# Block products with seven multiplications for three of five down-projection steps of the last layer's second token group

## The chip, the cores and the metric

The kernel runs on one core of one Trainium2 chip. The metric is the device time of one execution in microseconds (us): the median of several runs of the whole program, which is one launch.

## What is computed

The reference is one inference step of a two-layer decoder, D_MODEL = 1024, for a prompt of 1024 tokens and 8 sample tokens that share all weights. Layer 0 mixes by a gated linear recurrence and by attention to 256 memory tokens; layer 1 by stick-breaking attention over one shared K/V and by memory attention. After each mixer comes a SwiGLU feed-forward network with D_FF = 2816. All of it is float32.

```
h = h + rmsnorm(mix, g[1])
h = h + rmsnorm(swiglu(rmsnorm(h, g[2]), w_gu[l], w_down[l]), g[3])
```

Here `swiglu(x, w_gu, w_down)` is `(silu(x @ gate) * (x @ up)) @ w_down`. The change concerns the product with `w_down`, (2816, 1024), in layer 1.

## The kernel before

Tokens run in two groups along the free axis: group 0 has 512 prompt tokens, group 1 has the other 512 and the 8 sample tokens, 520 columns. Activations are held transposed, 128 features by tokens. A float32 product is made of three matmuls: each operand is split into a high part, rounded by a copy on ACT, and the rest, subtracted on DVE, and high x high, high x low and low x high are added in PSUM (`split_w` L256 for weights, `split_to` L286 for activations). So each weight block costs one load on SP's queue (256 KB for four blocks of 128x128), one cast on ACT, one subtraction on DVE, and its matmuls.

The order of the work is written by hand as generators: `weave` (L234) takes steps of several streams in the ratio of their weights, `drain` runs one after another. A planner then walks the program in that priority and places each instruction on its engine's queue when it judges it ready and a buffer of its pool free; queues run in order on the chip. Buffers rotate within a tag: `wraw` and `wspl` 5 each for loaded and split weights, tag "t" 3, tag "n" 2, tag "b" 7, "m" 5, the small tag "rr" 3, and from L1627 on four PSUM tags q0 to q3 with 2 banks each.

The feed-forward network works through the 22 blocks of D_FF in five parts of 5, 5, 4, 4 and 4 (`PARTS`, L642): the gate/up products of a part, then its share of the down projection, added into R.

The **last part** of the program is `ffn_w` (L644) for layer 1, group 1, started at L1628 and drained at L1629 and L1630. It splits the 520 columns into halves of 260. Four blocks are done plainly (`gate_up_q`, L528); the other 18 by `gate_up_w` (L553), which takes the gate and up weights as a 2 x 2 block matrix against the two column halves and needs seven block products in place of eight (the Winograd form of Strassen's scheme). Four of the seven use sums of weight blocks. These are made in DRAM ahead of time by `weight_sums` (L617): 8 steps for each part, each a small ACT copy of a value that the running work produces (a token), a POOL copy of the token, and a POOL-issued DMA from DRAM to DRAM that copies or accumulates. Steps are woven at L1606 and L1607 beside layer 1's first group. The sums of the activations are made by `sums_w` (L355). The sum of one product is carried to the next in PSUM by a negating ACT copy (L588, L591), and DVE combines (L599, L601).

The down projection of a part (L689 to L705) goes over the 8 output blocks: `split_w` for the 4 or 5 weight blocks, then for each block three matmuls on each half (L696), then two additions into R from PSUM on DVE (L705), or two copies in part 0 (L703). That is 192 or 240 matmuls of 260 columns a part.

The **recurrence** that the change touches is `a1.core()` (L1355, `hgrn_prompt` L1213), layer 0 group 1, woven at L1589 with part 0 of layer 0's network for group 0. `ffn` (L717) keeps its latest result as `self.now` for tokens.

At the start of the program the masks are built through buffers of tag "t" (L167), and the page table is loaded into a buffer of its own (L210, L211); it is used for indirect loads (L1018) in layer 1.

Of the kernel before, what the change touches and what calls it, by code (L numbers as in the profile page):

```python
# [9 lines left out]
F32 = mybir.dt.float32  # L10
# [8 lines left out]
P = 128  # L19
# [5 lines left out]
def tile_decoder(  # L25
# [50 lines left out]
    def T(dt=F32):  # L76
        return tpool.tile([P, WID], dt, tag="t", name=nm("t"))
# [20 lines left out]
    def M(dt=F32):  # L98
        return mpool.tile([P, 2, WID], dt, tag="m", name=nm("m"))
# [21 lines left out]
    def small(shape, dt=F32, tag="sm", bufs=None):  # L121
        return spool.tile(shape, dt, tag=tag, name=nm(tag), bufs=bufs)
# [86 lines left out]

    ptb = const.tile([P, NB * NP], I32, name="ptb")  # L210
    nc.sync.dma_start(ptb, page_table.rearrange("b j -> (b j)").partition_broadcast(P))  # L211
# [13 lines left out]
    def drain(*gens):  # L225
        for g_ in gens:
            for _ in g_:
                pass
# [5 lines left out]
    def weave(*streams):  # L234
        drain(mixed(*streams))
# [50 lines left out]
    def split_to(dst, src):  # L286
        nc.scalar.copy(dst[0], src)  # L287
        nc.vector.tensor_sub(dst[1], src, dst[0].bitcast(F32))  # L288
# [263 lines left out]

    def gate_up_w(l, f, ops, spl, raws):  # L553

# [37 lines left out]
        product(pa, 3)  # L592
        sg = T()
        nc.scalar.activation(sg[:, :h], pa[:, :h], AF.Silu)
# [10 lines left out]
        nc.vector.tensor_mul(sg[:, h:n], sg[:, h:n], gt[:, h:n])  # L605
        mt = M(F32R)
        split_to((mt[:, 0, :n], mt[:, 1, :n]), sg[:, :n])
        return mt

# [6 lines left out]

    def weight_sums(l, parts, after):  # L617

        for i in parts:
            f0, nf = PARTS[i]  # L620
            w = nf * P
            s1, s2, s3, s4 = (tc.dram_tile([512, w], F32, name=nm("wsum")) for _ in range(4))
            sums.setdefault(l, {})[i] = (s1, s2, s3, s4)
            a11, a12 = (w_gu[l][r : r + 512, f0 * P : f0 * P + w] for r in (0, 512))
            a21, a22 = (w_gu[l][r : r + 512, DFF + f0 * P : DFF + f0 * P + w] for r in (0, 512))
            for d, a, add in (
                (s3, a11, False), (s1, a21, False), (s3, a21, True), (s1, a22, True),
                (s2, s3, False), (s2, a22, True), (s4, s2, False), (s4, a12, True),
            ):
                tok = small([P, 1], tag="rr")  # L630
                nc.scalar.copy(tok, after())
                mark = nc.gpsimd.tensor_copy(small([P, 1], tag="mk", bufs=1), tok)
                with tc.issue_after(mark.ins):
                    if add:
                        nc.gpsimd.dma_start(d, a, accum_op=ALU.add)
                    else:
                        nc.gpsimd.dma_start(d, a, max_dma_last_dim=4 * w)
                yield

    htok = []  # L640

    PARTS = [(0, 5), (5, 5), (10, 4), (14, 4), (18, 4)]  # L642

    class ffn_w:  # L644


        def __init__(self, l, x, plain):
            self.g, self.l, self.x, self.ops, self.plain, self.n, self.r, self.pi = 1, l, x, [], plain, 0, 0, 0
            self.R = self.acc = None
            self.half = []  # L650
            self.sums = sums_w(x, self.ops)
# [15 lines left out]

        def part(self, pi):
            l, n, h = self.l, NG[1], PW[1]
            f0, nf = PARTS[pi]  # L670
            last = pi == len(PARTS) - 1
            mids = []
            for j in range(nf):
                self.pi = pi
                if f0 + j < self.plain:
                    mt, ins = gate_up_q(l, f0 + j, self.x)
                    mids.append(mt)
                    with tc.issue_after(ins.ins):
                        for _ in range((1, 2, 1, 0)[j]):
                            next(self.sums, None)  # L680
                else:
                    mids.append(gate_up_w(l, f0 + j, self.ops, self.spl, self.raws))
                yield
            if pi == 0:
                self.R = R_one()
            if last:
                self.acc = small([P, WID], tag="st", bufs=3)
                nc.scalar.preload_act_table_set("natural_log_exp_and_others")
            for m in range(ND):  # L689
                w = split_w(w_down[l], f0, nf, m * P)  # L690
# [897 lines left out]
    f0 = ffn(0, 0, o0.x)  # L1588
    weave((a1.core(), 22), (f0.part(0), 9))  # L1589
    a1.open()  # L1590
# [72 lines left out]
```

## Time and profile before

| | us |
|---|---|
| median of 3 runs | 2450.96 |
| lowest, highest run | 2450.86, 2453.5 |
| profiled execution | 2454.44 |
| its span in the trace | 2452.7 |

The profile is of one execution; its span is what the instructions cover, and 1.74 us of its time lie around it. Engines are PE (matmul), PEld (weight load, beside PE), DVE, ACT, POOL and SP, which issues loads. A busy PE may wait in its pipeline, so the pace of its matmuls is read beside its share. In the last part `q<-x,ws` and `q<-y,ws` at L581 are gate/up products and `q<-m,ws` at L696 is the down projection; L571/L572 and L266/L267 are cast and subtraction of the weight split.

### The profile page before, as it was taken

The numbers are of one execution on the slowest core, as the hardware profiler recorded it, in microseconds if no ns is written. First come the engines' busy times: TensorE is split into PE (matmuls) and PEld (weight loads), VectorE is DVE, ScalarE is ACT, GpSimd is POOL, SyncE is SP. The second block draws the span as 40 slices with busy tenths as digits, with TensorE's granted clock in tenths as the row PEclk, the third lists the DMA queues.
The fourth block names the chain that finished last, engine by engine and source line by source line (L and its number), as shares of the span: only waits on it lengthen the run. The fifth ranks groups of instructions, "written<-read, shape, count | busy, mean of one in ns | idle before, by whom it ended". The sixth has DMA issues, their size and how long they took to land.

```text
span 2452.7 us, 40619 instructions
## 1 busy us (share of the span) xinstructions
PE 2413.9 (98%) x15473; PEld 2141.9 (87%) x15473; DVE 1563.8 (64%) x2697; ACT 1204.3 (49%) x2354; POOL 102.6 (4%) x153
## 2 busy tenths in 40 slices
PE   7999999999999999999999999999999999999998
PEld 5888988888877887999999989877787898999997
DVE  5777556765775676555544585677677558655665
ACT  4547544444444454555433454555454445564444
POOL 2000000000000000011111100022000000000000
PEclk9999999999999999999999999999999999999998
DMA  5353252263543446686688866453453244375541
GB/s 177 106 157 104 74 159 84 65 178 118 179 136 95 138 146 210 171 221 150 181 201 220 237 187 189 153 163 118 140 154 117 82 126 125 117 200 148 151 134 66
DMA packets 496726, 360.33 MB, mean 147 GB/s; under 512 B 19181, under 2 KB 443738, under 8 KB 496530
## 3 DMA queue, kind: packets, MB, share of 16 engines
q1 hardware_dynamic: 477970, 303.19, 41.2%
q0 software_dynamic: 18560, 54.53, 9.1%
q8 instruction: 122, 2.00, 0.3%
q14 instruction: 74, 0.61, 0.1%
HBM read 327.83 MB, written 75.96 MB: 165 GB/s over the span
## 4 chain that ended last, share of the span: by engine, by line
PE 90%; DVE 4%; DMA 2%; ACT 2%; issue 1%; SPq 0%; POOL 0%; DVEq 0%; ACTq 0%; POOLq 0%
PE mm L280 62%; PE q L581 7%; PE q L696 5%; PE q L539 2%; PE mm L1082 2%; PE s L932 1%; PE s L891 1%; PE s L1265 1%; PE mm L868 1%; PE s L1440 1%; PE mm L841 1%; DMA b<-qd 1%; PE s L1479 1%; PE s L918 1%; DVE ws L267 1%
## 5 line engine op out<-in xcount | busy, mean ns | idle before, releaser
L280 PE MATMUL mm<-x,ws 128*128 128x260 f32 (+1 forms) x7776 | 1330.4, 330 | 0.0
L280 PEld LDWEIGHTS mm<-x,ws 128*128 128x128 f32 x7776 | 1149.2, 188 | 142.9 <-issue 8.2
L266 ACT CAST ws<-w 128x512 fp32r<-128x512 f32 x712 | 420.1, 591 | 685.7 <-PE mm L280 563.6
L267 DVE TENSOR_TENSOR ws<-w,ws 128x512 fp32r<-128x512 f32 x712 | 462.1, 652 | 263.3 <-ACT ws L266 255.7
L280 PE MATMUL mm<-m,ws 128*128 128x512 f32 (+1 forms) x2112 | 393.1, 343 | 0.4 <-DVE r L476 0.4
L280 PEld LDWEIGHTS mm<-m,ws 128*128 128x128 f32 x2112 | 324.3, 189 | 47.3 <-issue 3.4
L696 PE MATMUL q<-m,ws 128*128 128x260 f32 x1056 | 128.8, 283 | 0.0
L696 PEld LDWEIGHTS q<-m,ws 128*128 128x128 f32 x1056 | 127.2, 188 | 0.4 <-ACT hT L514 0.2
L572 DVE TENSOR_TENSOR ws<-w,ws 128x512 fp32r<-128x512 f32 x126 | 86.5, 691 | 59.7 <-ACT ws L571 57.0
L581 PE MATMUL q<-y,ws 128*128 128x260 f32 x864 | 112.9, 283 | 0.0
L571 ACT CAST ws<-w 128x512 fp32r<-128x512 f32 x126 | 78.0, 621 | 67.9 <-PE q L696 27.4
L581 PEld LDWEIGHTS q<-y,ws 128*128 128x128 f32 x864 | 107.6, 188 | 0.0
L476 DVE TENSOR_TENSOR r<-r,mm 128x512 f32<-128x512 f32 (+1 forms) x96 | 66.0, 687 | 59.9 <-PE mm L280 58.8
L320 DVE TENSOR_SCALAR t<-mm 128x512 f32<-128x512 f32 (+1 forms) x74 | 51.2, 692 | 64.3 <-PE mm L280 64.3
L732 DVE TENSOR_TENSOR t<-t,mm 128x512 f32<-128x512 f32 (+1 forms) x66 | 45.5, 689 | 67.9 <-PE mm L280 67.4
L324 DVE TENSOR_TENSOR t<-t,t 128x512 f32<-128x512 f32 (+1 forms) x66 | 45.8, 694 | 65.7 <-ACT t L323 65.7
L581 PE MATMUL q<-x,ws 128*128 128x260 f32 x648 | 86.3, 282 | 0.0
L581 PEld LDWEIGHTS q<-x,ws 128*128 128x128 f32 x648 | 81.3, 188 | 0.0
L343 DVE TENSOR_TENSOR st<-st,n 128x512 f32<-128x512 f32 (+1 forms) x98 | 67.1, 691 | 6.5 <-ACT n L342 5.0
L287 ACT CAST m<-t 128x512 fp32r<-128x512 f32 (+1 forms) x88 | 54.9, 624 | 25.3 <-DVE t L732 16.5
L1018 POOL DMA_INDIRECT c<-in_cache_sb_k,pidx x16 | 16.4, 1026 | 1128.7 <-issue 919.7
L288 DVE TENSOR_TENSOR m<-t,m 128x512 fp32r<-128x512 f32 (+1 forms) x88 | 60.9, 692 | 2.6 <-ACT m L287 1.4
(356 smaller groups left out, 2513.0 us busy)
## 6 DMA issues: line engine op xcount, KB each, us to landing
w<-in_w_gu SPq DMA_DIRECT2D x334, 256.0 KB, 3.1
w<-in_w_down SPq DMA_DIRECT2D x160, 256.0 KB, 2.7
w<-in_w_in_a SPq DMA_DIRECT2D x80, 256.0 KB, 2.9
wsum<-in_w_gu POOLq DMA_DIRECT2D x18, 1024.0 KB, 8.9
w<-wsum SPq DMA_DIRECT2D x72, 256.0 KB, 3.5
w<-in_w_o SPq DMA_DIRECT2D x64, 256.0 KB, 2.7
wsum<-in_w_gu POOLq DMA_DIRECT2D x12, 1280.0 KB, 10.5
w<-in_w_mem_kv SPq DMA_DIRECT2D x32, 256.0 KB, 3.2
```

Of the source, the lines that this page charges most:

```text
L266: nc.scalar.copy(ws[:, 0, :n, :], raw[:, :n, :])
L267: nc.vector.tensor_sub(ws[:, 1, :n, :], raw[:, :n, :], ws[:, 0, :n, :].bitcast(F32))
L280: nc.tensor.matmul(ps[:, a, : PW[g]], wt, xt[k][:, xi, o : o + PW[g]], start=(k == 0 and wi == 0), stop=(k == nk - 1 and wi == 2),)
L287: nc.scalar.copy(dst[0], src)
L288: nc.vector.tensor_sub(dst[1], src, dst[0].bitcast(F32))
L320: nc.vector.tensor_scalar(sv(x, g), pv(ps, g), -44.0, None, op0=ALU.max)
L343: nc.vector.tensor_add(acc[:, :n], acc[:, :n], t[:, :n])
L476: nc.vector.tensor_add(dst, dst, pv(ps, g))
L571: nc.scalar.copy(w[:, 0, :], src)
L572: nc.vector.tensor_sub(w[:, 1, :], src, w[:, 0, :].bitcast(F32))
L581: nc.tensor.matmul(ps[:, :h], w[:, wj, k * P : (k + 1) * P], x[:, xi, :], start=(first and k == 0 and wi == 0), stop=(k == 3 and wi == 2), ...
L696: nc.tensor.matmul(pp[a][:, :h], wt, mids[k][:, xi, a * h : (a + 1) * h], start=(k == 0 and wi == 0), stop=(k == nf - 1 and wi == 2),)
```

## The change

For parts 1, 2 and 3 the down projection also takes seven block products. The four weight blocks of a part form a 2 x 2 block matrix: rows by the parity of the block (blocks 0 and 2, blocks 1 and 3), columns by the halves of the 1024 outputs; the activations form one by parity and by column halves. `down_w` does this in two groups of two output blocks for each half of the outputs, holding all eight PSUM banks; a product is 12 matmuls, fed by one 256 KB load and one split. The fifth block of part 1 is added plainly (`slice_of`). Results go into R by DVE additions, 12 in a group and 14 with the fifth block, and two negating ACT copies of two banks each join the products.

The sums of down weights are made in DRAM by `down_sums`, 24 token steps of 512 KB, woven beside the recurrence at L1589. The sums of activations are made by `gate_up_w` for pairs of blocks: the first of a pair splits half 0 and the difference of the halves, the second splits itself and three more sums (`put_sum`: a subtraction, an ACT cast, a subtraction, 260 columns each). One of part 3's gate/up steps now comes ahead of part 2's down projection, and one of part 4's ahead of part 3's. The gate/up sums of the four plain blocks of part 0 are left out. The page table and its index go through buffers of tag "t".

```diff
-    ptb = const.tile([P, NB * NP], I32, name="ptb")
+    ptb = tpool.tile([P, NB * NP], I32, tag="t", name="ptb")
...
-    iot = const.tile([P, NB * NP], I32, name="iot")
+    iot = tpool.tile([P, NB * NP], I32, tag="t", name="iot")
...
-    def gate_up_w(l, f, ops, spl, raws):
+    def gate_up_w(l, f, ops, spl, raws, pair=None):
...
-        sg = T()
+        sg = T() if pair is None else N()
...
         mt = M(F32R)
+
+        def put_sum(dst, d, a, b):
+            nc.vector.tensor_sub(d, a, b)
+            split_to((dst[:, 0], dst[:, 1]), d)
+
+        if not pair:
+            w = n if pair is None else h
+            split_to((mt[:, 0, :w], mt[:, 1, :w]), sg[:, :w])
+            if pair is not None:
+                put_sum(mt[:, :, h:n], sg[:, :h], sg[:, h:n], sg[:, :h])
+                pair.append((mt, sg))
+            return mt
+        m0, s0 = pair.pop()
         split_to((mt[:, 0, :n], mt[:, 1, :n]), sg[:, :n])
+        y = [bpool.tile([P, 2, h], F32R, tag="b", name=nm("ys")) for _ in range(3)]
+        put_sum(y[2], s0[:, h:n], s0[:, h:n], sg[:, h:n])
+        put_sum(y[1], sg[:, h:n], sg[:, h:n], s0[:, :h])
+        put_sum(y[0], sg[:, :h], sg[:, :h], sg[:, h:n])
+        pair.extend((m0[:, :, :h], mt[:, :, :h], mt[:, :, h:n], y[0], m0[:, :, h:n], y[1], y[2]))
         return mt
...
-    def weight_sums(l, parts, after):
+    def weight_sums(l, parts, after, plain=0):
...
+            skip = max(0, plain - f0) * P
...
+            s1, s2, s3, s4 = (t[:, skip:w] for t in (s1, s2, s3, s4))
+            yield from summed((s1, s2, s3, s4), a11, a12, a21, a22, after)
+
+    def down_blocks(l, f0):
+        rows = w_down[l][f0 * P : (f0 + 4) * P, :].rearrange("(t s p) m -> s p t m", s=2, p=P)
+        return [rows[i][:, :, o : o + 512] for o in (0, 512) for i in range(2)]
+
+    def down_sums(l, parts, after):
+        for i in parts:
+            t = [tc.dram_tile([P, 2, 512], F32, name=nm("dsum")) for _ in range(4)]
+            dsums[i] = t
+            yield from summed(t, *down_blocks(l, PARTS[i][0]), after)
+
+    def summed(t, a11, a12, a21, a22, after):
...
+            tok = small([P, 1], tag="rr")
+            nc.scalar.copy(tok, after())
+            mark = nc.gpsimd.tensor_copy(small([P, 1], tag="mk", bufs=1), tok)
+            with tc.issue_after(mark.ins):
+                if add:
+                    nc.gpsimd.dma_start(d, a, accum_op=ALU.add)
+                else:
+                    nc.gpsimd.dma_start(d, a, max_dma_last_dim=4 * 512)
+            yield
...
+        def down_w(self, pi, f0, pairs, extra):
...
+            src = ((a11, 0), (s1, 4), (s2, 5), (a12, 1), (s3, 6), (s4, 2), (a22, 3))
+            for m0 in (0, 2):
+                ms = (m0, m0 + 1)
+                acc = [[Q(i) for i in range(4)] for _ in ms]
...
+                def product(q, j, first=False):
+                    w = weight(src[j][0])
+                    for i in range(2):
+                        for t in range(2):
+                            x = pairs[t][src[j][1]]
+                            o = t * 256 + i * P
+                            for wi, (wj, xi) in enumerate(((0, 0), (0, 1), (1, 0))):
+                                nc.tensor.matmul(
+                                    acc[i][q][:, :h], w[:, wj, o : o + P], x[:, xi, :],
+                                    start=(first and t == 0 and wi == 0), stop=(t == 1 and wi == 2),
+                                    skip_group_check=True,
+                                )
...
+                product(0, 0, True)
+                minus(1, 0)
+                product(3, 1, True)
+                product(1, 2)
+                minus(2, 1)
+                product(0, 3)
+                if extra:
+                    tail = w_down[l][(f0 + 4) * P : (f0 + 5) * P, :].rearrange("p (o m) -> p o m", o=2)
+                    we = weight(tail)
+                    slice_of(0, 0, 0)
+                add(3, 4, 1)
+                add(0, 0, 0)
+                product(1, 4)
+                add(3, 0, 1, True)
+                add(1, 4, 1)
+                product(2, 5)
+                if extra:
+                    slice_of(2, 0, 1)
+                add(2, 0, 1)
+                product(1, 6)
+                if extra:
+                    slice_of(1, 1, 0)
+                    slice_of(0, 1, 1, True)
+                    add(0, 4, 1)
+                add(1, 4, 0)
+                yield
...
-    weave((a1.core(), 22), (f0.part(0), 9))
+    weave((a1.core(), 22), (f0.part(0), 9), (down_sums(1, (1, 2, 3), lambda: f0.now), 24))
...
-    ws = weight_sums(1, range(5), lambda: f1.now)
+    ws = weight_sums(1, range(5), lambda: f1.now, 4)
...
-    drain(f1.part(2), f1.part(3), f1.part(4), f1.finish_rows())
+    drain(f1.gate_up(2), f1.gate_up(3, 0, 1), f1.down(2), f1.gate_up(3, 1))
+    drain(f1.gate_up(4, 0, 1), f1.down(3), f1.gate_up(4, 1), f1.down(4), f1.finish_rows())
```

More of the change, by code (lines that the diff above doesn't have):

```diff
@@ L623, in weight_sums @@
             sums.setdefault(l, {})[i] = (s1, s2, s3, s4)
[L624 to L638, printed above, removed]
+            c0, c1 = f0 * P + skip, f0 * P + w
@@ L649, in __init__ @@
             self.R = self.acc = None
-            self.half = []
+            self.half, self.mids = [], {}
             self.sums = sums_w(x, self.ops)
@@ L684, in part, with down @@
+        def down(self, pi):
+            l, n, h = self.l, NG[1], PW[1]
+            f0, nf = PARTS[pi]
+            last = pi == len(PARTS) - 1
+            mids, pairs = self.mids.pop(pi)
             if pi == 0:
@@ L688, in part @@
                 nc.scalar.preload_act_table_set("natural_log_exp_and_others")
+            if self.block(pi):
+                yield from self.down_w(pi, f0, pairs, mids[4:])
+                return
             for m in range(ND):
```

45 lines of the change are left out of this document (41 added, 4 removed).

## The prediction

> **What bounds the kernel now.** I read the page first: busy time by engine, then the span in 40 slices.
>
> ```profile
> span 2452.7 us, 40619 instructions
> ...
> PE 2413.9 (98%) x15473; PEld 2141.9 (87%) x15473; DVE 1563.8 (64%) x2697; ACT 1204.3 (49%) x2354; POOL 102.6 (4%) x153
> ...
> PE   7999999999999999999999999999999999999998
> ...
> PEclk9999999999999999999999999999999999999998
> ```
>
> PE is busy almost everywhere and its granted clock is full, but a busy PE here need not be at its peak. So next comes the chain of waits for the last part, where the change removes work (columns: start, length, piece):
>
> ```profile
> 2164.42 50.43 PE q L581 x420
> 2214.85 28.70 PE q L696 x240
> 2243.55 40.34 PE q L581 x336
> 2283.89 22.99 PE q L696 x192
> 2306.89 40.37 PE q L581 x336
> 2347.26 23.03 PE q L696 x192
> ...
> 2436.38 0.02 issue
> 2436.40 0.77 DVE r L705 x2
> ```
>
> The reader is to see that nothing but PE stands in the chain over the three steps: each is a gate/up piece (L581) followed by a down piece (L696), without a wait. The pace is the same in both: 28.70/240 = 0.1196, 22.99/192 = 0.1197, 23.03/192 = 0.1199, and 50.43/420 = 0.1201 us a matmul of 260 columns. That is what one matmul is worth here. The same stretches in the table by stage:
>
> ```profile
> core 0: us, PE busy (x) PEld busy (x) DVE busy (x) ACT busy (x) POOL busy (x), PEclk, DMA share, GB/s
> 2214.85:2243.55 28.70, 28.70 (x242) 28.70 (x242) 15.67 (x35) 10.19 (x20) 0.00 (x0) 1.00 0.44 128
> 2243.55:2283.89 40.34, 40.34 (x339) 40.34 (x338) 26.57 (x48) 24.32 (x50) 0.00 (x0) 1.00 0.62 181
> 2283.89:2306.89 23.00, 23.00 (x195) 23.00 (x194) 12.96 (x27) 6.22 (x10) 0.00 (x0) 1.00 0.40 117
> ```
>
> PE has no gap; DVE is at 55 to 66%, ACT at 27 to 60%. So fewer matmuls shorten the end one for one, until DVE or ACT cannot follow. That is the question of this change.
>
> **What it removes.** One matmul here is one 128x128 weight block times 260 columns. A down step of 4 blocks has 4 x 8 x 3 x 2 = 192 of them (240 with 5). In down_w one product is 2 x 2 x 3 = 12, seven products are 84, two column groups 168; the fifth block of part 1 adds 2 x 24 = 48, so 216. Each of parts 1, 2, 3 loses 24: 24 x (0.1196 + 0.1197 + 0.1199) = **8.62 us** gone from PE.
>
> **What it adds in the last part**, priced by the groups of the last 300 us:
>
> ```profile
> L572 DVE TENSOR_TENSOR ws<-w,ws 128x512 fp32r<-128x512 f32 x119 | 81.8, 691 | 56.4 <-ACT ws L571 53.8 <-DMA w<-in_w_down 1.6
> L571 ACT CAST ws<-w 128x512 fp32r<-128x512 f32 x119 | 73.6, 621 | 61.7 <-PE q L696 27.4 <-PE q L581 19.8 <-DMA w<-wsum 6.6
> L705 DVE TENSOR_TENSOR r<-r,q 128x260 f32<-128x260 f32 x64 | 24.4, 421 | 29.0 <-PE q L696 28.9
> L288 DVE TENSOR_TENSOR m<-t,m 128x520 fp32r<-128x520 f32 x17 | 11.9, 699 | 1.4 <-ACT m L287 1.4
> L605 DVE TENSOR_TENSOR t<-t,t 128x260 f32<-128x260 f32 x17 | 7.2, 423 | 1.0 <-ACT t L603 1.0
> L588 ACT ACTIVATE q<-q 128x260 f32<-128x260 f32 x17 | 6.3, 372 | 5.4 <-PE q L581 5.4
> ```
>
> A duration is not what an operation takes from DVE when another stands behind it:
>
> ```profile
> 2218.36 0.76 DVE L705 TENSOR_TENSOR r<-r,q 128x260 f32<-128x260 f32 x2
> 2240.56 1.29 DVE L572 TENSOR_TENSOR ws<-w,ws 128x512 fp32r<-128x512 f32 x2
> ```
>
> Two adds of 0.42 end after 0.76, two splits of 0.69 after 1.29: spacings of 0.34 and 0.60. I work with these, and keep the durations as the other end.
>
> - A column group of parts 2 and 3 (84 matmuls, 84 x 0.1198 = 10.06 us of PE) asks DVE for 7 splits and 12 adds: 7 x 0.60 + 12 x 0.34 = 8.3 us; ACT for 7 casts and 4 negations: 7 x 0.62 + 4 x 0.37 = 5.8. With the fifth block: 8 splits and 14 adds, 9.6 against 108 x 0.1198 = 12.9.
> - A gate/up step that completes a pair (also 84 matmuls) has 7 splits, four small vector operations, the 520-wide split, and three put_sums of two 260-wide operations: 4.2 + 10 x 0.34 + 0.6 = 8.2 of 10.06. One that opens a pair needs 6.6 (the wide split becomes three 260-wide operations).
>
> By duration six pairs (3.1 us each) and three down steps (8.2, 7.5, 7.5) add some 42 us to DVE, near the limit but not over it, which PE covers as long as split weights lie ready: there are 5 buffers of wspl plus some of cpool, a product uses one, so DVE may be late by 5 to 7 us.
>
> Loads: 14 of 256 KB for 8 in parts 2 and 3, 16 for 16 in part 1. A down group then loads 7 per 84 matmuls, as gate/up already does at a DMA share of 0.62 without a gap on PE: nothing. SP issues them in the same mix: nothing.
>
> New waits on PE: the negation of the first product's sum, which the third product adds to, has the whole second product (12 matmuls, 1.44 us) as cover for 2 x 0.37 on ACT, as L588 has now. Behind the last matmuls of part 1's group stands one bank that the next group needs first; its two adds follow PE's end by 0.02 and take 0.77 (chain above). Half of that lies under the second bank's matmuls, but a split in front costs 0.69: 0.1 to 0.8 us, at two places. I take **0.8 us** for all stalls, the middle; the ends are 0 and what the DVE rival gives. Putting the first step of the next part's gate/up ahead of parts 2's and 3's down steps moves no work, only hides pair sums.
>
> **What it adds in the recurrence.** 24 more tokens (ACT copy, POOL copy, POOL-issued DMA of 512 KB) beside a1.core and f0.part(0). Rows of the existing sums, then that stage and a plain 512 KB load:
>
> ```profile
> L631 ACT COPY rr<-t x22: 184/186/191, 1001.6 to 1389.3; 128x1 f32<-128x1 f32 x22
> L632 POOL COPY mk<-rr x40: 184/548/694, 1001.9 to 1415.4; 128x1 f32<-128x1 f32 x40
> L635 POOL DMA_DIRECT2D wsum<-in_w_gu x20: 998/1026/1102, 1027.0 to 1421.0; - x20
> DMA to landing us min/median/max: 8.7/9.7/13.5
> L637 POOL DMA_DIRECT2D wsum<-wsum x10: 652/658/776, 1055.3 to 1414.7; - x10
> DMA to landing us min/median/max: 5.3/6.7/9.8
> 387.00:500.00 113.00, 112.78 (x600) 94.57 (x600) 75.51 (x158) 51.14 (x103) 0.00 (x0) 1.00 0.26 75
> c<-in_cache_mem_k SPq DMA_DIRECT2D x16, 512.0 KB, 4.4
> ```
>
> ACT pays 24 x 0.19 = 4.5 us where it is busy 51 of 113; POOL (24 x (0.55 + 0.85) = 34 us) is idle there. DMA share 0.26 leaves room. Cover: PE has 112.78 of 113. I take nothing. The bound above is a wait, not work: three token buffers, so ACT's fourth token waits for POOL, and all weight casts stand behind it. That is the slow rival.
>
> **Smaller edits.** The gate/up sums of part 0 shrink from 1280 to 256 KB an issue; PE is full there even at the highest DMA share, so nothing is won:
>
> ```profile
> 1070.00:1100.00 30.00, 29.63 (x239) 28.57 (x238) 16.32 (x30) 16.76 (x39) 3.75 (x6) 1.00 0.97 257
> ```
>
> The page table's load now waits for a buffer that the mask building turns over:
>
> ```profile
> 4.92 0.63 SPq L211 DMA_DIRECT2D ptb<-in_page_table  x1
> 17.77 0.20 DVE L177 CAST mask<-mf 128x64 uint8<-128x64 f32 x1 [0.44 <-POOL mf L173]
> 19.26 1.53 SPq L1074 DMA_DIRECT2D w<-in_w_in_a  x3
> 54.07 0.69 DVE L1135 SCALAR_TENSOR_TENSOR t<-t 128x512 f32<-128x512 f32 x1 [2.10 <-ACT t L1133]
> ```
>
> It can issue at about 16 to 18 us. If it stands in SP's queue before the five early weight loads (5.60 on), these would go 12 us later and PE, which starts its projection at 19.9, with them; the planner orders by readiness (this iota runs at 1.05, ahead of lines above it), so I put it in the gap before 19.26. The t buffers are next used at 54. Zero, with up to +10 in the slower cases.
>
> **Sum.** -8.62 + 0.8 = -7.8 us. The profiled execution took 2454.44 (span 2452.7) and would take 2446.6; the median, 3.48 lower, goes from 2450.96 to **2443.2 us**.
>
> **Rivals.**
>
> 1. *DVE paces the new blocks.* If an operation costs its whole duration and 0.04 us of hand-over (19 operations, 0.8 us), a group of parts 2 and 3 needs 7 x 0.69 + 12 x 0.42 + 0.8 = 10.7 for 10.06, and a pair-closing step 4.8 + 10 x 0.42 + 0.7 + 0.8 = 10.5. Four groups at 0.6 and six steps at 0.45 give back 5.1 us: 2448.3. Against it: the spacings 0.34 and 0.60; for it: in-order queues, and adds that wait for PE with splits behind them. The Trainium skill (VectorE: DVE Perf Modes, "The DRAIN you can't avoid") says that the next DVE operation cannot issue until the pipe of the one before is empty, though it points on to a section where one that is not held starts earlier. By the strict reading this rival holds; the trace disagrees, with two adds of 0.42 in 0.76. Chance 0.14.
> 2. *The sums fall behind beside the recurrence (slower).* A part's sums are 8 steps, of which five landings follow one another. 24 steps in 113 us give a part 37 us, and three spare tokens of 4.7 us add 14 over all three parts, or 4.7 a part. It decides when five landings exceed 42 us: 8.4 each. The rows above, for 1024 to 1280 KB, give 6.7 + 9.7 + 6.7 + 9.7 + 6.7 = 39.5; half the bytes should be well below (4.4 for the plain 512 KB load). If they landed like the worst rows (9.8 and 13.5, 56 us a part), ACT would be held 3 x 19 - 14 = 43 us; a mean overrun of a third of this, 14 us, gives 2457. Chance 0.09.
> 3. *The planner redraws the rest.* The order of every queue comes from a list plan; 24 new ACT and POOL operations and moved buffers can shift it from 387 us on, and PE's idle time (2452.7 - 2413.9 = 38.8 us) with it. A tenth of that lost, 4 us: 2447; as much as all the gain, 2451. Chance 0.10.
> 4. *It does not do what it says*: PE keeps its time although the matmuls go, since weights of sums from DRAM come late. L571 waits 6.6 us for wsum loads now, all in slack. That would give 2451. Chance 0.03.
>
> **Chances and range.** Forecast case 0.60, holding 2441.5 to 2446; 0.04 for less than that (no stall, plan luckier: 2450.96 - 8.62 = 2442.3 less 2). Rivals 0.14, 0.09, 0.10, 0.03. A measurement of this kernel can tell about 0.2%, 4.9 us, from no change. Faster by more (under 2446.1): 0.60 + 0.04 + a third of rival 3 and a little of rival 1, 0.70. Within: 0.20, of rivals 1, 3 and 4. Slower (over 2455.9): rival 2 and the late page table, 0.10. For 8 in 10 the range takes in rival 1 and most of rival 3: 2440.5 to 2451.
>
> **What would show it.** Right: in the chain of waits the three down pieces of the last part have 216, 168 and 168 matmuls and take 25.9, 20.1 and 20.1 us without DVE or ACT pieces between; DVE there 75 to 85% busy. Rival 1: DVE over 90% there, and idle PE released by the weight split or the add into r. Rival 2: in the recurrence, ACT idle before the token copy, released by POOL, and PE busy less than 112 of 113. Rival 3: the last part shorter by 8, and the recurrence or the turn into the last part longer. Wrong altogether would be a pace other than 0.12 us a matmul in the new blocks.

## The result, and the profile after

The changed kernel takes 2445.15 us (median of 20 runs, 2441.79 to 2449.93) against 2452.06 us for the kernel before (20 runs, 2450.07 to 2455.52). The ratio is 0.9974 with a 95% interval of [0.9967, 0.9980], so between 4.9 and 8.1 us are gained. The prediction was 2443.2 us, a gain of 7.8 (the two medians are 6.9 apart).

The profiled execution took 2445.71 us. First its page, with the lines that were shown of before:

```profile
span 2443.6 us, 40814 instructions
...
PE 2403.0 (98%) x15401; PEld 2131.2 (87%) x15401; DVE 1598.5 (65%) x2785; ACT 1229.1 (50%) x2438; POOL 132.5 (5%) x201
...
PE   7999999999999999999999999999999999999997
...
PEclk9999999999999999999999999999999999999999
```

PE lost 72 matmuls and 10.9 us of busy time, and its share did not fall. The span is 9.1 us shorter; where, the chain of waits of the last part says (start, length, piece; L581 is gate/up as before, L760 the block products, L748 the fifth block, L822 the plain down projection, L831 its additions):

```profile
2163.26 50.46 PE q L581 x420
2213.72 5.77 PE q L760 x48
...
2226.77 5.83 PE q L760 x48
...
2238.42 1.46 PE q L748 x12
2239.88 50.54 PE q L581 x420
2290.42 20.13 PE q L760 x168
2310.55 40.37 PE q L581 x336
2350.92 20.06 PE q L760 x168
2370.98 30.26 PE q L581 x252
...
2426.94 0.77 DVE r L831 x2
```

Again only PE stands in it. Part 1's down piece runs from 2213.72 to 2239.88: 26.16 us for 216 matmuls. Parts 2 and 3 have 168 each in 20.13 and 20.06. That is 0.1211, 0.1198 and 0.1194 us a matmul: the pace of before, a little slower in part 1. The order of gate/up and down pieces is another one, but their sum can be compared. Here is the whole stretch from the first gate/up product of part 1 to the last addition in the table by stage, before and then after:

```profile
2164.42:2436.40 271.98, 271.97 (x2265) 271.39 (x2265) 163.06 (x307) 139.20 (x275) 0.00 (x0) 1.00 0.46 134
```

```profile
2163.26:2426.94 263.68, 263.67 (x2193) 263.10 (x2193) 197.75 (x394) 162.30 (x335) 0.00 (x0) 1.00 0.54 156
2213.72:2239.88 26.16, 26.16 (x218) 26.16 (x218) 20.98 (x45) 12.95 (x25) 0.00 (x0) 1.00 0.61 173
2290.42:2310.55 20.13, 20.13 (x171) 20.13 (x170) 18.57 (x42) 11.90 (x24) 0.00 (x0) 1.00 0.66 188
387.00:500.00 113.00, 112.73 (x599) 94.44 (x599) 75.08 (x157) 53.31 (x127) 25.94 (x45) 1.00 0.74 176
```

The reader is to see four things. The last part went from 271.98 to 263.68 us: **8.30 us** for 72 matmuls. PE has no gap in it. DVE rose from 60% to 75%, and stands at 92% in part 2's down piece (18.57 of 20.13), still with no gap on PE (part 3: 18.28 of 20.06). And beside the recurrence (387 to 500) the DMA share rose from 0.26 to 0.74, while PE kept 112.73 of 113 us (112.78 before).

The rest of the difference in span, 0.8 us, is no effect that can be named: 1.16 us are gained up to 2163, and 0.36 lost behind the last addition. The kernels below that are the same as the changed one up to the last part enter it between 2161.94 and 2165.23 (the rows of two of them are shown with their experiments).

### The profile page after: what moved, and what is told of

Its sections match the earlier page's. It is cut to its first block, busy times and chain, and to the rows that moved or that the text cites. A ratio compares the mean times of both kernels' runs of the same rounds, so it can differ in the third digit from the quotient of the medians.

```text
span 2443.6 us, 40814 instructions
## 1 busy us (share of the span) xinstructions
PE 2403.0 (98%) x15401; PEld 2131.2 (87%) x15401; DVE 1598.5 (65%) x2785; ACT 1229.1 (50%) x2438; POOL 132.5 (5%) x201
## 4 chain that ended last, share of the span: by engine, by line
PE 89%; DVE 4%; DMA 2%; ACT 2%; issue 1%; SPq 0%; POOL 0%; DVEq 0%; ACTq 0%; POOLq 0%
PE mm L280 61%; PE q L581 7%; PE q L760 2%; PE q L822 2%; PE q L539 2%; PE mm L1208 2%; PE s L1058 1%; PE s L1017 1%; PE s L1391 1%; PE mm L994 1%; PE s L1566 1%; PE mm L967 1%; DMA b<-qd 1%; PE s L1605 1%; DVE ws L267 1%
## 5 line engine op out<-in xcount | busy, mean ns | idle before, releaser
L266 ACT CAST ws<-w 128x512 fp32r<-128x512 f32 (+1 forms) x680 | 402.6, 593 | 653.1 <-PE mm L280 558.0
L267 DVE TENSOR_TENSOR ws<-w,ws 128x512 fp32r<-128x512 f32 (+1 forms) x680 | 443.4, 655 | 242.9 <-ACT ws L266 237.7
L572 DVE TENSOR_TENSOR ws<-w,ws 128x512 fp32r<-128x512 f32 x126 | 86.6, 691 | 46.4 <-ACT ws L571 43.5
L581 PE MATMUL q<-y,ws 128*128 128x260 f32 x864 | 112.7, 283 | 0.0
L581 PEld LDWEIGHTS q<-y,ws 128*128 128x128 f32 x864 | 107.3, 188 | 0.0
L571 ACT CAST ws<-w 128x512 fp32r<-128x512 f32 x126 | 77.8, 618 | 47.2 <-PE q L581 15.2
L581 PE MATMUL q<-x,ws 128*128 128x260 f32 x648 | 86.9, 283 | 0.0
L581 PEld LDWEIGHTS q<-x,ws 128*128 128x128 f32 x648 | 81.7, 189 | 0.0
L667 POOL COPY mk<-rr 128x1 f32<-128x1 f32 x64 | 29.3, 458 | 751.3 <-ACT rr L666 751.3
L321 ACT ACTIVATE t<-t 128x512 f32<-128x512 f32 (+1 forms) x66 | 41.9, 635 | 40.7 <-DVE t L320 36.3
L287 ACT CAST m<-t 128x512 fp32r<-128x512 f32 (+1 forms) x76 | 47.4, 623 | 25.3 <-DVE t L858 18.0
L822 PE MATMUL q<-m,ws 128*128 128x260 f32 x432 | 53.6, 284 | 0.0
L288 DVE TENSOR_TENSOR m<-t,m 128x512 fp32r<-128x512 f32 (+1 forms) x76 | 52.5, 691 | 1.2
```

The lines of the kernel that those rows point to most:

```text
L266: nc.scalar.copy(ws[:, 0, :n, :], raw[:, :n, :])
L267: nc.vector.tensor_sub(ws[:, 1, :n, :], raw[:, :n, :], ws[:, 0, :n, :].bitcast(F32))
L571: nc.scalar.copy(w[:, 0, :], src)
L572: nc.vector.tensor_sub(w[:, 1, :], src, w[:, 0, :].bitcast(F32))
L581: nc.tensor.matmul(ps[:, :h], w[:, wj, k * P : (k + 1) * P], x[:, xi, :], start=(first and k == 0 and wi == 0), stop=(k == 3 and wi == 2), ...
L822: nc.tensor.matmul(pp[a][:, :h], wt, mids[k][:, xi, a * h : (a + 1) * h], start=(k == 0 and wi == 0), stop=(k == nf - 1 and wi == 2),)
```

## The experiments

The theory: PE sets the pace of the last part, so 72 matmuls at 0.12 us go one for one, and DVE follows because operations in a row cost their spacing. The rivals of the prediction: DVE paces the new blocks, the sums hold ACT through the three token buffers, the planner redraws the rest. Each experiment is one edit; the ratio is to the kernel before. Those that start from the changed kernel are to be read beside its 0.9974.

**1. The sums alone**, put into the kernel before and not used:

```diff
-    weave((a1.core(), 22), (f0.part(0), 9))
+    weave((a1.core(), 22), (f0.part(0), 9), (down_sums(1, (1, 2, 3), lambda: f0.now), 24))
```

> The kernel before, with the 24 token steps that make the sums of down weights beside the recurrence, and nothing else; no one reads the sums. My theory (they hide): the stretch 387 to 500 us stays within 0.5 us of before, total 0 to +0.5 us, ratio 1.0000 to 1.0002. Rival 2 (the sums fall behind and hold ACT): ACT idle before token copies until POOL is done, total +2 us or more. Rival 3 (the plan of the rest is redrawn): a shift of 1 to 4 us either way that lies outside 387 to 510 us.

Measured: 2452.83 us, ratio 1.0002 [0.9993, 1.0011]; PE in 387 to 500 is 112.71 us. The sums cost nothing that can be measured (the interval is 2 us to either side), and the planner, given the 24 steps, does not lose the rest of the program. So the rival by which it redraws the rest is not seen; 1 or 2 us of it would not be either.

**2. The block products without the sums**:

```diff
-            s1, s2, s3, s4 = dsums[pi]
+            s1, s2, s3, s4 = a12, a21, a22, a11
...
-    weave((a1.core(), 22), (f0.part(0), 9), (down_sums(1, (1, 2, 3), lambda: f0.now), 24))
+    weave((a1.core(), 22), (f0.part(0), 9))
```

> The changed kernel without the sums: the 24 token steps are left out, and the block products load plain weight blocks in the place of the four sums, so the down projection of parts 1 to 3 comes out as another matrix; all matmuls, splits, additions and loads of the last part are there. My theory: from the first gate/up product of part 1 to the last addition 263.7 us as in the changed kernel (271.98 before), total 2443.5 to 2445, that is at most 1.5 us under the changed kernel. Rival 2: what the sums cost comes back here, 2 us or more under the changed kernel. If sums from DRAM came late in the last part (rival 4), that part itself gets shorter than 263.7.

Measured: 2445.40 us, 0.9970 [0.9958, 0.9982]; the last part runs from 2164.13 to 2427.81, 263.7 us. Without the sums the gain is the same as with them, as far as these runs can tell (the interval is 3 us to either side). So it comes from the last part, and the recurrence takes nothing of it that can be measured. The last part is as long with plain weight blocks in the place of the sums, so sums that come late from DRAM, the prediction's fourth rival, are ruled out too.

**3. The small edits alone** (page table and index in tag "t", smaller gate/up sums of part 0), in the kernel before:

```diff
-    ptb = const.tile([P, NB * NP], I32, name="ptb")
+    ptb = tpool.tile([P, NB * NP], I32, tag="t", name="ptb")
...
-    ws = weight_sums(1, range(5), lambda: f1.now)
+    ws = weight_sums(1, range(5), lambda: f1.now, 4)
```

> The kernel before, with the small edits alone: page table and index in buffers of tag t, and no gate/up sums for the four plain blocks of part 0. My theory: PE's first projection starts about 0.9 us earlier as in the changed kernel's trace, and the total is within 1 us of before. Rival 3: these edits alone move it by 1 to 3 us, since the plan of the first 400 us differs.

Measured: 2452.83 us, 1.0000 [0.9991, 1.0009]. The total is as expected. The first projection was not: it began at 20.2 us, where the kernel before has 19.9 and the changed one 19.0.

**4. Four more DVE operations in each column group**: a value is subtracted from R and added again.

```diff
-                def add(q, mo, a, sub=False):
+                def add(q, mo, a, sub=False, again=False):
...
+                        if again:
+                            nc.vector.tensor_sub(d, d, acc[i][q][:, :h])
+                            nc.vector.tensor_add(d, d, acc[i][q][:, :h])
...
-                add(0, 0, 0)
+                add(0, 0, 0, again=True)
```

> The changed kernel with 4 more 260-wide vector operations in each of the six column groups (the same PSUM value is subtracted and added again). My theory (an operation takes its spacing, 0.34 us, and DVE has room): a group of parts 2 and 3 needs 8.3 + 1.4 = 9.7 of 10.06 us, so the last part grows by 0 to 1 us. Rival 1 (it takes its duration and the hand-over): 10.7 + 4 x 0.46 = 12.5 for 10.06, so four groups grow by 1.8 us each over the changed kernel and the last part by 7 us, with PE idle before L760 until DVE.

Measured: 2445.02 us, 0.9970 [0.9960, 0.9981]. The last part in the table by stage:

```profile
2161.94:2425.64 263.70, 263.69 (x2193) 263.12 (x2193) 204.12 (x418) 162.23 (x335) 0.00 (x0) 1.00 0.54 156
```

24 operations more on DVE, and 263.70 us, where the changed kernel has 263.68. If a vector operation took its whole duration of its engine, the groups of parts 2 and 3 would already have been full, and these would have come on top. The first rival falls.

**5. Twelve more**, by the same edit on three of the additions:

```diff
-                add(3, 4, 1)
-                add(0, 0, 0)
+                add(3, 4, 1, again=True)
+                add(0, 0, 0, again=True)
...
-                add(1, 4, 1)
+                add(1, 4, 1, again=True)
```

> The changed kernel with 12 more 260-wide vector operations in each of the six column groups. My theory (spacing 0.34 us): a group of parts 2 and 3 needs 8.3 + 4.1 = 12.4 us of DVE for 10.06 of PE, one of part 1 13.7 for 12.9; 4 x 2.3 + 2 x 0.8 = 10.8 us, less what split weights in stock cover: the last part grows by 4 to 11 us, with PE idle released by DVE. By durations and hand-over (rival 1): 16.2 for 10.06 and 17.8 for 12.9: 34 us. If it grows by less than 4 us, DVE has more room than I worked out.

Measured: 2455.22 us, 1.0012 [1.0002, 1.0021]. The table by stage, then PE's largest wait in that stretch (waiting engine and line, and whom it waits for: us, times, longest), then the chain in part 1's down piece:

```profile
2165.23:2437.20 271.97, 266.47 (x2192) 263.59 (x2191) 219.09 (x466) 161.89 (x335) 0.00 (x0) 1.00 0.53 151
```

```profile
PE q L760 <- DVE r L772: 3.2, 3, 1.3
```

```profile
2234.90 0.79 DVE r L769 x2
2235.70 0.67 DVE r L771 x2
```

To its last addition at 2437.43 the part takes 272.2 us, 8.5 more than in the changed kernel. Now PE waits for DVE, and DVE stands in the chain. Two operations of 0.42 us take 0.67: a spacing of 0.335. By spacings, 8.5 us was within what was expected (4 to 11); by durations it would have been 34. So DVE's limit exists and lies between four and twelve operations a group. The strict reading of the Trainium skill (VectorE: DVE Perf Modes, "The DRAIN you can't avoid"), by which the next operation does not start until the pipe is empty, does not hold in these rows; they fit the remark there that a next operation which is not held starts earlier.

**6. Sums of twice the bytes** (1024 KB a step; only the first half of each is used):

```diff
-    def down_blocks(l, f0):
-        rows = w_down[l][f0 * P : (f0 + 4) * P, :].rearrange("(t s p) m -> s p t m", s=2, p=P)
+    def down_blocks(l, f0, nb=4):
+        rows = w_down[l][f0 * P : (f0 + nb) * P, :].rearrange("(t s p) m -> s p t m", s=2, p=P)
...
-            t = [tc.dram_tile([P, 2, 512], F32, name=nm("dsum")) for _ in range(4)]
-            dsums[i] = t
-            yield from summed(t, *down_blocks(l, PARTS[i][0]), after)
+            t = [tc.dram_tile([P, 4, 512], F32, name=nm("dsum")) for _ in range(4)]
+            dsums[i] = [x[:, :2] for x in t]
+            yield from summed(t, *down_blocks(l, PARTS[i][0], 8), after)
```

> The changed kernel with sums of twice the size: each of the 24 transfers beside the recurrence moves 1024 KB; only the first half is used. Rival 2 decides here: five landings of 8.4 us or more a part overrun the 42 us that a part has. By the rows of 1024 KB sums (6.7 and 9.7) I expect 40 to 48 us a part. If ACT is held by the three token buffers, the recurrence (its last product at 507 to 508 us) ends 3 to 15 us later and so does the whole; if the planner has put the tokens late enough, or the sums just run on past the recurrence, nothing moves (under 1 us).

Measured: 2474.46 us, 1.0088 [1.0072, 1.0103]. The recurrence ends at 531.5 us in place of 508.1. I had expected 3 to 15 us; it is 23 there, and some 28 in the total by the ratios. The chain of waits shows how, and the waits of 480 to 510 its size:

```profile
500.89 1.20 POOL dsum L670
502.09 0.20 POOL mk L667
...
502.31 0.19 ACT rr L666
...
502.52 0.59 ACT b L1424
...
503.16 2.08 PE s L1428 x8
```

```profile
ACT rr L666 <- POOL mk L667: 20.4, 3, 8.5
POOL dsum L670 <- DMA dsum<-dsum: 15.3, 2, 8.3
...
PE s L1428 <- ACT b L1424: 12.8, 1, 12.8
```

POOL stands on the landing of a sum before it may issue the next; the mark (L667) stands behind it; ACT's token (L666) waits for the mark of three tokens ago; and the recurrence's own ACT operation (L1424) stands behind the token, with PE behind that. This is the slow rival's mechanism. In the changed kernel POOL waits for landings as well (387 to 510), but among its waits there is none of ACT for POOL:

```profile
POOL dsum L670 <- DMA dsum<-dsum: 23.1, 5, 5.7
```

The difference is the landing. The lists of issues give its median (last column, us) in the changed kernel and here:

```profile
dsum<-in_w_down POOLq DMA_DIRECT2D x18, 512.0 KB, 6.5
...
dsum<-dsum POOLq DMA_DIRECT2D x6, 512.0 KB, 4.8
```

```profile
dsum<-in_w_down POOLq DMA_DIRECT2D x18, 1024.0 KB, 11.3
...
dsum<-dsum POOLq DMA_DIRECT2D x6, 1024.0 KB, 8.8
```

Of the five landings that follow one another in a part's sums, three are of the first kind and two of the second: 3 x 6.5 + 2 x 4.8 = 29 us against 3 x 11.3 + 2 x 8.8 = 52 us. The prediction put the turning point at 42, but it shared out the 113 us of the whole stretch. The tokens of the changed kernel start between 400.7 and 493.0 us, one in 4.0 us. That gives a part 32 us, and the three spare tokens add 4: an estimate of some 36, still between 29 and 52.

**7. The old order of the last steps**:

```diff
-    drain(f1.gate_up(2), f1.gate_up(3, 0, 1), f1.down(2), f1.gate_up(3, 1))
-    drain(f1.gate_up(4, 0, 1), f1.down(3), f1.gate_up(4, 1), f1.down(4), f1.finish_rows())
+    drain(f1.part(2), f1.part(3), f1.part(4), f1.finish_rows())
```

> The changed kernel with the steps of the last part in their old order: part 2's down projection right behind its gate/up steps, then part 3's, no gate/up step of the next part ahead. My theory: the pair sums of the last two blocks (three sums, about 5 us of ACT and DVE behind the last product) then stand in front of the third product of the down projection, which comes 2.9 us after: 2 us each at parts 2 and 3, so the last part grows by 3 to 5 us. If the move was worth nothing, 0.

Measured: 2444.90 us, 0.9973 [0.9961, 0.9985]. From the first gate/up product of part 2 to the first of part 4's plain down products it takes 161.91 us (2239.19 to 2401.10), against 161.36 (2239.88 to 2401.24). I had expected 3 to 5 us; that fell. The chain shows how close it is, at part 2 and then at part 3:

```profile
2239.19 40.43 PE q L581 x336
2279.62 3.34 PE q L760 x28
2282.97 0.03 issue
2283.00 17.01 PE q L760 x140
...
2343.30 0.42 ACT ys L287
...
2343.76 16.99 PE q L760 x140
```

At part 2 PE goes from gate/up into the down piece without a wait that shows. At part 3 the pair sums do stand in the chain, from 2338.94 on, as I had expected. But PE is busy for 161.82 of the 161.91 us: the first two products need none of the last three sums and take 2.9 us, and the cast of the one sum that the third needs is over 3.3 us after the end of gate/up at part 2, where I had counted 5 for all three. The pair sums come almost in time, and the order written by hand hides 0.55 us here.

**8. Part 0 too by block products**, with 32 sums beside the recurrence:

```diff
-            return 0 < pi < len(PARTS) - 1
+            return pi < len(PARTS) - 1
...
+                        if pi == 0 and (m + mo, a) not in seen:
+                            seen.add((m + mo, a))
+                            nc.scalar.activation(d, acc[i][q][:, :h], AF.Copy, scale=-1.0 if sub else 1.0)
+                            continue
...
-    weave((a1.core(), 22), (f0.part(0), 9), (down_sums(1, (1, 2, 3), lambda: f0.now), 24))
+    weave((a1.core(), 22), (f0.part(0), 9), (down_sums(1, (0, 1, 2, 3), lambda: f0.now), 32))
```

> The changed kernel with part 0's down projection as block products too: four more pairs of sums of activations in the plain gate/up steps, first touches of R as ACT copies, 8 more token steps (32) beside the recurrence. My theory: 24 matmuls less, 2.87 us, and 0 to 0.5 us more for the sums: 2442 to 2443. Rival: part 0 shares DVE with the sums of the inputs and the other group's finish (62 of 93 us busy there), and the gain is lost: 2445 or more, with idle PE between 2070 and 2165 us.

Measured: 2459.51 us, 1.0040 [1.0026, 1.0053]. I had expected 2442 to 2443, and feared for DVE in part 0; neither came. Eight more sums of 512 KB are enough for the slow rival. In experiment 10, where nothing holds the 32 tokens, they start between 399.1 and 491.5 us, one in 3.0 us, so a part has some 26 us (an estimate, with its share of the spare tokens). Its five landings take 3 x 6.7 + 2 x 4.7 = 29.5 us by the medians of this run. PE has 20.22 of 30 us in 480 to 510 (29.73 in the changed kernel), ACT's token waits for POOL again, and the recurrence ends at 520.1. The last part does not win either: from part 0's first plain product to the last addition it takes 357.8 us, against 358.0. Part 0 saves 2.9 us up to 2172, and then part 1's gate/up piece loses 2.8, with weight loads in the chain:

```profile
2172.28 4.42 DMA w<-in_w_gu
...
2177.33 5.32 DMA w<-in_w_gu
```

**9. Experiment 6 with a token of its own for each step** (a column of a constant that is no longer needed then), so that ACT waits for no mark:

```diff
+    own = [flip[:, k : k + 1] for k in range(24)]
...
-            tok = small([P, 1], tag="rr")
+            if own:
+                tok = own.pop()
+            else:
+                tok = small([P, 1], tag="rr")
```

> The kernel with sums of 1024 KB, but each of the 24 tokens beside the recurrence has a place of its own (a column of a tile that is free by then) in the place of three shared buffers, so ACT never waits for POOL. If the three buffers are what turned slow sums into 29 us over the changed kernel, the recurrence ends at 507 to 509 us again, PE's clock stays at 1.00 there, and the time is 2444 to 2448 (a rest for 24 more megabytes of traffic). If the traffic itself holds the weight loads, PE still idles between 480 and 530 us and 10 us or more remain.

Measured: 2465.84 us, 1.0054 [1.0039, 1.0070]. The recurrence ends at 510.2, not 531.5: the three buffers account for 21 of the 23 us there. But the total falls by only 8.6 us, and it is still some 20 above the changed kernel (1.0054 against 0.9974). The sums go on behind the recurrence as in experiment 6, with issues up to 547 us, and in the stretch after it PE idles under a high DMA share, and the granted clock (in front of the DMA share) is below 1:

```profile
510.00:540.00 30.00, 25.72 (x113) 20.30 (x112) 15.50 (x21) 11.57 (x20) 4.43 (x8) 0.94 1.08 260
540.00:580.00 40.00, 33.46 (x182) 26.92 (x181) 21.30 (x30) 14.22 (x24) 1.15 (x1) 0.91 0.89 250
```

In 510 to 580 us PE waits 9.4 us for DVE (L863), and DVE 14.1 us for loads of the sample tokens' state (L1314), where it waits 5.3 us for them in the changed kernel. So at twice the bytes there are two costs: the hold on ACT, and the traffic itself, which appears when the hold is taken away.

**10. Experiment 8 with 32 tokens of their own**, and part 0 woven later beside the end of group 0:

```diff
-    weave((chain(f0.finish(False), store_y(0, f0.R), token_rows(1, o1.R)), 17), (chain(f1.part(0), f1.part(1)), 7))
+    weave((chain(f0.finish(False), store_y(0, f0.R), token_rows(1, o1.R)), 17), (chain(f1.part(0), f1.part(1)), 5))
```

> Part 0 as block products too (32 tokens), with a place of its own for every token, and the rows and the other group's finish woven earlier into part 0 (17 to 5 in the place of 17 to 7). My theory: the recurrence is as in the changed kernel (end at 508), the last part from its first plain product to the last addition takes 355 to 356 us (358.0 in the changed kernel), the time is 2442 to 2443. Rival: DVE is full there and part 1 starts late, as with part 0 alone, and the last part keeps 358 or more.

Measured: 2447.99 us, 0.9984 [0.9975, 0.9993]. The recurrence is whole again (end at 506.6, PE 29.65 of 30 in 480 to 510), and the last part takes 356.7 us, 1.3 less than 358.0. I had expected 355 to 356 and a total of 2442 to 2443; the total is no better than the changed kernel's. A part of the gain is lost behind the recurrence, where the transfers of 32 sums run on:

```profile
510.00:540.00 30.00, 28.92 (x138) 22.85 (x137) 21.24 (x28) 12.46 (x22) 3.38 (x7) 1.00 1.04 273
```

PE has all 30 us there in the changed kernel, at a DMA share of 0.82.

**11. The changed kernel with free tokens and one DRAM tile for all twelve sums**, against the time outside the span (below):

```diff
-            t = [tc.dram_tile([P, 2, 512], F32, name=nm("dsum")) for _ in range(4)]
+            if not dall:
+                dall.append(tc.dram_tile([P, 2, 12 * 512], F32, name="dsums"))
+            t = [dall[0][:, :, o : o + 512] for o in range(4 * (i - 1) * 512, 4 * i * 512, 512)]
```

> The changed kernel with a place of its own for every token and with one DRAM tile for all twelve sums. Kernels with the twelve tiles took 2.1 us beside their span, those without 1.7: if that is the number of tiles, 1.7 to 1.8 here, and with the tokens off the chain of the recurrence the time is 0.4 to 0.8 us under the changed kernel; if it is the DRAM size or the traffic, 2.1 stays.

Measured: 2445.05 us, 0.9972 [0.9961, 0.9984]; 2.16 us outside the span, as with twelve tiles. The number of tiles is not its cause, and at 512 KB and 24 steps free tokens are worth nothing that can be measured.

**12. Experiment 10 with its 32 sums in two places**, 16 beside the recurrence and 16 beside parts 2 and 3 of the network that follows:

```diff
-    weave((a1.core(), 22), (f0.part(0), 9), (down_sums(1, (0, 1, 2, 3), lambda: f0.now), 32))
+    ds = down_sums(1, (0, 1, 2, 3), lambda: f0.now)
+    weave((a1.core(), 22), (f0.part(0), 9), (islice(ds, 16), 16))
...
-    weave((chain(a1.merge(), a1.mem()), 12), (a1.mem_sample(), 20), (chain(f0.part(2), f0.part(3)), 16))
+    weave((chain(a1.merge(), a1.mem()), 12), (a1.mem_sample(), 20), (chain(f0.part(2), f0.part(3)), 16), (ds, 16))
```

> Part 0 as block products with a place for every token, and of the 32 token steps 16 stand beside the recurrence and 16 beside parts 2 and 3 of the same network (some 150 us later, DMA share 0.3 to 0.6). If the load of 32 sums on the transfers behind the recurrence was what took the gain of part 0, the stretch 387 to 540 is as in the changed kernel and the time is 2442 to 2444; if the last part's own gain of 1.3 us is all there is, 2444 to 2446, which a run cannot tell from the changed kernel.

Measured: 2449.85 us, 0.9990 [0.9981, 0.9999], above both of the ranges that I had given. The stretch behind the recurrence is free again (PE 30.00 of 30 in 510 to 540), but the second place is not, in the table by stage:

```profile
540.00:700.00 160.00, 156.55 (x795) 128.12 (x794) 108.31 (x170) 65.76 (x129) 10.40 (x16) 0.99 0.64 180
700.00:850.00 150.00, 147.74 (x713) 117.89 (x712) 88.11 (x141) 65.72 (x132) 10.25 (x16) 1.00 0.51 143
```

PE has 159.09 and 150.00 us there in the changed kernel, so 2.5 and 2.3 us are lost, more than part 0 brings. No version that was run beats the changed kernel.

## Why the prediction was right

The mechanism was right, and the time lies in the range, 2 us above the forecast. 1.1 us of these two are the kernel before itself, which the prediction took at 2450.96 and which has a median of 2452.06 in the 20 runs. The sign of being right was met in the chain: the three down pieces were to take 25.9, 20.1 and 20.1 us, and they take 26.16, 20.13 and 20.06, with no piece of DVE or ACT between. Step by step:

- **PE's saving, 8.62 us.** Right. 72 matmuls went at the same pace, and the last part is 8.30 us shorter. Experiment 2 has the gain without the sums, experiment 1 the sums without the gain.
- **Stalls, 0.8 us.** Mis-sized: 8.62 - 8.30 = 0.32 us were given back. Nearly all of it stands in part 1's down piece, 26.16 against 216 x 0.1197 = 25.86, but not at the two short places that the prediction named. At the turn between the two groups the first 48 matmuls take 5.83 us, where those of the first group have 5.77; behind the second group, the next gate/up piece takes 50.54 us, where part 1's has 50.46. The rest is spread over the piece; why its pace is slower there stays open.
- **DVE follows, by spacings and not by durations.** Right, and decided by experiments 4 and 5, from both sides. The mark that the prediction set for the first rival, "DVE over 90% there, and idle PE", was half met: 92% and 91% in the down pieces of parts 2 and 3, no idle PE. So the prediction's own sign, 75 to 85%, held in part 1 alone (80%). A busy share made of durations that overlap says little about room: with experiment 4's additions it is 19.00 of 20.14 us in part 2's down piece, and the length is the same. The work added to DVE is 34.7 us by busy time, where 42 had been forecast from durations: busy time counts the overlap once.
- **The sums beside the recurrence, nothing.** Right in the total (experiment 1), but with less room than "DMA share 0.26 leaves room" says: the share rose to 0.74, and a third more sums already held the recurrence by 12 us (experiment 8). The condition that the prediction gave for the slow rival, five landings against the time that a part has, was the right one, but its turning point was too high. By the prediction's count a part has 42 us with 24 steps and 31 with 32 (28, and 3 for the spare tokens), and landings of 29.5 would have been free with 32. By the times of the tokens it is some 36 and 26 us, and that sorts the cases: 29 in the changed kernel, 52 with twice the bytes, 29.5 with 32 steps. The price, 14 us, came near with 32 steps by luck (1.0040 against 0.9974, some 16 us), since it was a third of a hold by the slowest landings. It is half of what twice the bytes cost (1.0088, some 28 us): it had only the hold in it and not the traffic behind it.
- **The order of the pieces, nothing.** Right; my later belief that it is worth 3 to 5 us fell with experiment 7.
- **The small edits, nothing.** Right in the total (experiment 3), wrong in the place. SP's queue of the changed kernel at the start:

```profile
5.02 2.08 SPq L1200 DMA_DIRECT2D w<-in_w_in_a  x4
15.29 0.33 SPq L211 DMA_DIRECT2D ptb<-in_page_table  x1
15.66 1.75 SPq L1200 DMA_DIRECT2D w<-in_w_in_a  x2
```

  SP stands on the page table's buffer for 8.1 us, and the fifth of the five early weight loads goes behind it, at 15.66, where the prediction had all five ahead of it. It did no harm here: four weights were issued ahead of it, and the first projection starts at 19.0 us, not later than the 19.9 of before.
- **What was not in the sum.** The time outside the span: 2.17 us in the changed kernel, 1.74 before, so 0.43 us are given back that no row of the profile shows. The three kernels without sums (before, experiments 2 and 3) have 1.70 to 1.74; those with 24 sums of 512 KB (1, 4, 5, 7, 11 and the changed kernel) 2.15 to 2.17; with 24 of 1024 KB (6 and 9) 1.91; with 32 of 512 KB (8, 10, 12) again 1.70 to 1.73. Only kernels with sums have more than 1.74, but it does not grow with their number or bytes; its cause stays open.

Together: 8.30 - 0.43 = 7.9 us, at the upper end of what was measured (4.9 to 8.1). The kernels with a last part of about the same length (2, 4, 7 and 11) have ratios of 0.9970 to 0.9973, 6.6 to 7.4 us. The chain of the changed kernel has two tokens of 0.19 us in the recurrence that the kernel before does not have, and they may be a part of the rest. About a microsecond is not explained; a single profile cannot resolve it, since kernels of the same code enter the last part 3.3 us apart.

## What to carry to other kernels

Where PE stands alone in the chain of waits, matmuls removed go one for one at the pace read from that chain, and the question is only whether the other engines keep up: price them by the spacing of operations that follow one another, as read from the trace, not by their durations or busy share. A side stream whose steps are released by an in-order engine is free until its landings take longer than its tokens last; then the whole engine stands behind it, and the step from free to 12 us was a third more sums here. Read from the trace when the tokens really come, in place of sharing out the length of the stretch. Taking away the hold does not take away the traffic, so look at what comes after.

## What was not expected of the hardware

The granted clock fell when PE stood still, and came back late. In experiment 6 PE works until 480.7 us and then waits, at first until 485.8; one-microsecond rows of the table by stage:

```profile
484.00:485.00 1.00, 0.00 (x0) 0.00 (x0) 0.00 (x0) 0.94 (x4) 0.18 (x1) 0.74 0.67 39
485.00:486.00 1.00, 0.17 (x1) 0.17 (x2) 0.19 (x1) 0.95 (x4) 0.00 (x0) 0.50 0.86 98
...
508.00:509.00 1.00, 1.00 (x7) 0.91 (x6) 0.00 (x0) 0.39 (x1) 0.00 (x0) 0.82 1.17 260
```

The clock (third column from the right) fell to 0.50 some 3.8 us after the last matmul. It stayed there through a little work between 485.8 and 490.3 and through the wait of 12.8 us that followed. Work resumed at 503.16 and ran at half pace, eight matmuls of L1428 in 2.08 us where the changed kernel's chain has 1.16, until about 508.4: 5 us. So this wait of PE cost about 2.6 us more than its own length, an estimate from half of these 5.2 us. In experiment 9 a gap of 1.9 us (480.9 to 482.8) was followed by a fall, a microsecond after work had begun again:

```profile
482.00:483.00 1.00, 0.19 (x1) 0.19 (x2) 0.22 (x2) 0.82 (x3) 0.00 (x0) 1.00 0.96 115
483.00:484.00 1.00, 1.00 (x10) 1.00 (x10) 0.00 (x0) 0.00 (x0) 0.00 (x0) 0.95 0.89 152
484.00:485.00 1.00, 1.00 (x7) 1.00 (x7) 0.92 (x3) 0.00 (x0) 0.00 (x0) 0.50 1.14 206
```

The Trainium skill (TensorE: Matmul & The Clock Gate, "Part 1: The HAM clock gate (the "warmup" mystery)") has the clock halve after an idle window of about 3.4 us and return after about as much sustained work. Experiment 6 agrees roughly, with 3.8 and 5 us; the fall after a gap of 1.9 us in experiment 9 is not covered by that window.
